# A mixer that begins with the memory's keys, its norm beside them, and low products that come last

## The chip, the cores and the metric

The kernel runs on one core of one Trainium2 chip. The metric is the time of one execution on the device, in microseconds (us), as the median of three runs. TensorE is called PE (its weight loads PEld), VectorE DVE, ScalarE ACT, GpSimd POOL and SyncE SP, as in the profile.

## What is computed

One inference step of a decoder trunk with two layers, in float32, for 256 prompt tokens and 8 x 8 sample tokens, which stand side by side as T = 320 columns. The model width is 1024, the hidden width of an FFN 2816, and there are 256 memory tokens, four heads, a pooling mixer in four groups and a causal depthwise convolution with 31 taps. The core of a layer:

```
x = x + 0.5 * swiglu_ffn(rmsnorm(x, ffn1_norm), ffn1_w_gu, ffn1_w_down)
h = rmsnorm(x, mix_norm)
u, v, q, gl = split(h @ w_in)
y_pool = pool_mixer(u)                # window means minus token, per-group map
a, gate = split(v);  z = a * sigmoid(gate)
y_conv = silu(layernorm(depthwise_conv31(z) + b_dw)) @ w_pw
k, v = split(rmsnorm(mem, mem_g) @ w_kv)        # keys and values of the memory
y_att  = cross_attend(q, k, v)
gates  = sigmoid(gl)                            # one per branch and channel
merged = gates[0]*y_pool + gates[1]*y_conv + gates[2]*y_att
x = x + merged @ w_out
x = x + 0.5 * swiglu_ffn(rmsnorm(x, ffn2_norm), ffn2_w_gu, ffn2_w_down)
```

A final RMSNorm follows. The sample group has cached keys, values, pool and conv states of its own; the new keys, values and states are outputs too.

## The kernel before

**Products in three parts.** Each operand is split into a high part (rounded to the type fp32r) and a low part, the rest. A product of a 128x128 block of weights with 320 columns of activations is three matmuls: high weight by high activation (L294), high weight by low activation (L295), low weight by high activation (L296). `chain` (L291) adds up such blocks in one PSUM bank, block after block, with the three parts of each block in turn. Banks are `mm` (three), `cv` and `st` (two each) and `sa`.

**Weights** come from DRAM in chunks of 1 MB, 16 blocks, on SP's queue, into four `raw` buffers, in the order that `stream_plan` lists; the memory tokens (`"m"`) and cached keys and values (`"k"`, `"v"`) have places in the same list. A *unit* is half a chunk: 8 blocks, 1024 columns. `Stream.split` makes its two halves `whi` and `wlo`: ACT casts `whi` (L224) and DVE subtracts for `wlo` (L116, the helper that issues all of DVE's work and all of POOL's arithmetic). While `share` is set, which is from the start of a mixer to ahead of `w_pw`, the second unit of each chunk goes another way: ACT casts `whi` (L217), ACT writes the rounded weights, negated, into `wlo` (L218), and a DMA from POOL's queue adds the weights themselves there, so that the low part stays (L219, `wlo<-in_w` in the trace). Four `whi` and four `wlo` buffers exist, and units are split three ahead of the one in use (`LA`).

**What runs beside the products.** At each new unit, `unit()` runs functions put off by `defer`, splits the next unit, and lets side tasks (generators begun by `start` with a rate) go on by so many steps. The convolution is the largest: 31 taps for each of 8 channel blocks on 256 columns and on the samples, on DVE, with a share on POOL and PE (`diag` products), paced at `RC` = 2.5 steps per unit. The tile scheduler then fixes the order in which each engine's instructions stand, from the order of the code, the waits and the buffers.

**The order of a mixer** before: `z` (16 units: for each of 8 blocks a chain for `a` and one for the gate, on an `h` that is multiplied by its weight but not yet by 1/rms, so that `rstd` is multiplied in after the bank, as `za` and `sgv`); beside it the statistics' product and rsqrt, and the memory operands `memh`, `meml` (`mem_operands`); the memory's keys (`kv_keys`, 8 units, result `kt`) and values (`kv_values`, 8 units, L457 on, line L471 for its low product) with `norm_gen` beside, which makes the normalised operands `hhi`, `hlo` of the rest; `q` (8 units); four pooling groups, with the attention's scores between them and the gates A; the gates C and B (8 units each; B's sigmoid is `sgb`, L847); the convolution's LayerNorm and SiLU (L566) and the operands `chi` (L567) and `clo`; the projection `w_pw` (8 units); and the output projection `w_out` (8 units) on the operands `mgh`, `mgl` of the merged branches. A mixer has 74 units ahead of `w_pw` in the stream. An FFN (`ffn`) has 44 units of gate and up products and 22 of the down product, and calls `on_block` as each block of the new `x` is done; at the end of FFN 1 that starts the norm's statistics and the operands of the un-normalised `h`.

In the profiled execution the mixer of layer 0 runs from 245.6 to 626 us (`z` to 312.6, keys to 343.4, the pooling groups from 402 to 503, gates C and B to 569, `w_pw` to 598), that of layer 1 from 1091.7 to 1476 us. The stretch from the start of `z` to the end of the pooling groups is called the stretch of the conv taps here.

## Time and profile before

| what | value |
|---|---|
| median of the three runs (lowest, highest) | 1725.13 us (1719.79, 1726.79) |
| profiled execution, its own time | 1725.18 us |
| its span in the trace | 1723.4 us |
| PE busy | 1654.5 us (96%) |
| DVE busy | 1119.0 us (65%) |
| ACT busy | 840.7 us (49%) |
| POOL busy | 319.8 us (19%) |
| DMA, mean of 16 engines | 187 GB/s |

Busy time counts an engine's instructions, which on PE overlap their successors, so that a busy PE is not PE at its best; what PE waits for, and the clock that it is granted (PEclk, 1.00 for 2.4 GHz), say more. Busy shares are means over stages with different limits: the four FFNs, some 230 us each, and the two mixers, 380 us each.

### The profile page before, as it was taken

Reading aid. Unit: us, or ns where it says so; the run is one execution under the profiler, and the core shown is the slowest. Engines: PE = TensorE matmul, PEld = TensorE weight load, DVE = VectorE, ACT = ScalarE, POOL = GpSimd, SP = SyncE. Lnnn points to the kernel's source line nnn. Section 1 sums busy time; section 2 is a strip of 40 time slices with the busy share of each in tenths; the row PEclk is TensorE's granted clock in tenths of the full one; section 3 lists DMA queues with packets and bytes.
Section 4 is the critical chain, followed back from the end, with each engine's and each line's share of the span. In section 5 each row is a group of like instructions: output and inputs, shape, how many; then the busy total and the mean of one; then the engine's idle time right before and its main releaser. Section 6 shows DMA issues by size and latency. Waiting matters only on the chain.

```text
span 1723.4 us, 27500 instructions
## 1 busy us (share of the span) xinstructions
PE 1654.5 (96%) x11194; PEld 1597.1 (93%) x11194; DVE 1119.0 (65%) x1822; ACT 840.7 (49%) x1267; POOL 319.8 (19%) x356
## 2 busy tenths in 40 slices
PE   8999998889999999999999999998899999999996
PEld 8999998879788999999999999997888899999996
DVE  7655449999754576564465555689995636755544
ACT  5444346656657354443344433555666664444432
POOL 2000005777410000000000000367762100000000
PEclk9999999999999999999999999999999999999999
DMA  7444457899899544444444444688888974444430
GB/s 266 147 147 152 152 185 214 219 256 253 251 293 273 176 151 155 147 147 148 147 147 150 153 155 154 180 230 230 227 266 269 311 208 161 147 150 154 155 129 31
DMA packets 51935, 322.52 MB, mean 187 GB/s; under 512 B 6240, under 2 KB 6304, under 8 KB 18656
## 3 DMA queue, kind: packets, MB, share of 16 engines
q1 hardware_dynamic: 38160, 270.75, 45.1%
q0 software_dynamic: 13360, 49.68, 13.5%
q8 instruction: 88, 1.44, 0.3%
q10 hardware_dynamic: 288, 0.33, 0.1%
q14 instruction: 39, 0.32, 0.1%
HBM read 311.91 MB, written 8.82 MB: 186 GB/s over the span
## 4 chain that ended last, share of the span: by engine, by line
PE 76%; DMA 9%; DVE 8%; issue 3%; POOL 2%; ACT 2%; DVEq 0%; SPq 0%; POOLq 0%; ACTq 0%
PE mm L296 17%; PE mm L294 17%; PE mm L295 17%; DMA wlo<-in_w 9%; PE cv L294 7%; PE cv L296 7%; PE cv L295 7%; DVE cv L116 3%; POOL pr L116 2%; DVE wlo L116 1%; PE sa L645 1%; DVE us L116 1%; PE st L825 1%; ACT wlo L218 1%; DVE hlo L116 0%
## 5 line engine op out<-in xcount | busy, mean ns | idle before, releaser
L224 ACT CAST whi<-raw 128x1024 fp32r<-128x1024 f32 (+1 forms) x371 | 388.3, 1047 | 601.5 <-PE mm L295 345.2
L116 DVE TENSOR_TENSOR wlo<-raw,whi 128x1024 fp32r<-128x1024 f32 (+1 forms) x371 | 465.3, 1254 | 242.5 <-ACT whi L224 241.6
L294 PE MATMUL mm<-hhi,whi 128*128 128x320 f32 x1736 | 547.0, 315 | 16.1 <-DVE sgv L116 9.6
L296 PE MATMUL mm<-hhi,wlo 128*128 128x320 f32 x1736 | 541.3, 313 | 16.4 <-DMA wlo<-in_w 16.3
L295 PE MATMUL mm<-hlo,whi 128*128 128x320 f32 x1736 | 542.0, 312 | 0.0
L294 PEld LDWEIGHTS mm<-hhi,whi 128*128 128x128 f32 x1736 | 329.3, 190 | 28.2 <-issue 15.5
L296 PEld LDWEIGHTS mm<-hhi,wlo 128*128 128x128 f32 x1736 | 328.9, 190 | 22.0 <-DMA wlo<-in_w 19.9
L295 PEld LDWEIGHTS mm<-hlo,whi 128*128 128x128 f32 x1736 | 329.4, 190 | 1.8 <-issue 0.4
L116 DVE SCALAR_TENSOR_TENSOR cv<-z,cst,cv 128x256 f32<-128x256 f32 x480 | 205.4, 478 | 3.4 <-ACT cv L484 1.4
L294 PE MATMUL cv<-hhi,whi 128*128 128x320 f32 x568 | 175.5, 309 | 0.0
L295 PE MATMUL cv<-hlo,whi 128*128 128x320 f32 x568 | 175.5, 309 | 0.0
L296 PE MATMUL cv<-hhi,wlo 128*128 128x320 f32 x568 | 175.5, 309 | 0.0
L116 POOL MEMSET z<- 128x120 f32 x4 | 0.8, 212 | 742.2 <-PE mm L295 742.2
L217 ACT CAST whi<-raw 128x1024 fp32r<-128x1024 f32 x74 | 77.5, 1048 | 120.3 <-PE mm L295 110.3
L294 PE MATMUL mm<-hidh,whi 128*128 128x320 f32 x418 | 129.2, 309 | 0.0
L295 PE MATMUL mm<-hidl,whi 128*128 128x320 f32 x418 | 129.2, 309 | 0.0
L296 PE MATMUL mm<-hidh,wlo 128*128 128x320 f32 x418 | 129.2, 309 | 0.0
L116 POOL TENSOR_TENSOR pr<-pr 128x512 f32<-128x512 f32 (+3 forms) x128 | 116.6, 911 | 6.6
L219 POOL DMA_DIRECT2D wlo<-in_w x74 | 64.6, 873 | 257.8 <-ACT wlo L218 188.5
L296 PEld LDWEIGHTS cv<-hhi,wlo 128*128 128x128 f32 x568 | 106.6, 188 | 0.0
L295 PEld LDWEIGHTS cv<-hlo,whi 128*128 128x128 f32 x568 | 106.6, 188 | 0.0
L294 PEld LDWEIGHTS cv<-hhi,whi 128*128 128x128 f32 x568 | 106.6, 188 | 0.0
(191 smaller groups left out, 2632.0 us busy)
## 6 DMA issues: line engine op xcount, KB each, us to landing
raw<-in_w SPq DMA_DIRECT2D x221, 1024.0 KB, 4.8
wlo<-in_w POOLq DMA_DIRECT2D x74, 512.0 KB, 8.9
raw<-in_kc SPq DMA_DIRECT2D x16, 1024.0 KB, 9.3
raw<-in_vc SPq DMA_DIRECT2D x16, 1024.0 KB, 8.7
out_co<-z POOLq DMA_DIRECT2D x16, 135.0 KB, 6.0
raw<-in_mem SPq DMA_DIRECT2D x2, 1024.0 KB, 4.8
out_mk<-kt POOLq DMA_DIRECT2D x2, 1024.0 KB, 9.4
out_mv<-va POOLq DMA_DIRECT2D x2, 1024.0 KB, 8.3
```

The costliest lines, as they stand in the source:

```text
L116: return op(*args, **kw)
L217: nc.scalar.copy(hi[:, :], raw)
L218: nc.scalar.mul(lo[:, :], raw, -1.0)
L219: nc.gpsimd.dma_start(lo[:, :], w_in[c][:, 1024:2048], accum_op=ALU.add)
L224: nc.scalar.copy(h, r)
L294: nc.tensor.matmul(out, hi, xh, start=(i == 0), stop=False)
L295: nc.tensor.matmul(out, hi, xl, start=False, stop=False)
L296: nc.tensor.matmul(out, lo, xh, start=False, stop=(i == len(xs) - 1))
L645: nc.tensor.matmul(po[32 * h:32 * h + 32, :256], pp[:, at:at + 32], raw[:, mb * 1024 + h * 256:mb * 1024 + h * 256 + 256], start=(bb == 0 ...
L825: nc.tensor.matmul(pv[:, :TP], vt[:, mb, o * P:o * P + P], kt[:, 2 * hd + mb, :], start=(mb == 0), stop=(mb == 1))
```

## The change

- The mixer begins with the memory's keys. `stream_plan` returns a list `seq` of chunks, in which the keys' four chunks stand ahead of those of `z`, and the values' behind; the memory tokens are loaded when FFN 1's down product begins, and their operands are made beside that product (`at_down`), with the subtraction on DVE where POOL had it.
- At the end of FFN 1 only the statistics are summed. `norm_gen` runs beside the keys from their third unit on, four steps a unit: DVE multiplies `x` by its weight and by `rstd` (`hf`), ACT casts `hhi`, DVE subtracts `hlo`.
- `z`'s chains take these normalised operands. The gate's sigmoid reads its bank, and `zfin` multiplies the other bank, which it holds until then, by the gate. `za`, the multiplications by `rstd` and the second set of operands are gone.
- In a chain all products with high halves of a unit come first, then those with its low halves; `kv_values` alike.
- While `share` is set, every third unit goes by way of the DMA, where it was every second: 48 such DMAs instead of 74 in the program, and 397 subtractions of `wlo` on DVE instead of 371.
- The pool `hp` goes, and the `big` buffers are eight instead of six.

Per mixer, DVE loses 16 multiplications by `rstd` and gains 8 `hf`; POOL loses 8 `hf` and 8 `meml`, and DVE gains the latter beside FFN 1. ACT has 26 loads of function tables instead of 34 in the program.

```diff
@@ -31,7 +31,7 @@
 NRAW = 4
 NW = 4
 LA = 3
-NBIG = 6
+NBIG = 8
 C_LEAD = 24
 RC = 2.5
 RS = 1.0
...
@@ -45,13 +45,24 @@
 C_ALL = C_ID + P
 
 
+LP = (2 * NJ * 24 + 720) // 16
+MP = NJ * 24 // 16
+
+
 def stream_plan():
 
+
     at = {}
+    seq = []
     nb = 0
     for l in range(L):
+        c = l * LP
+        seq += list(range(c, c + MP))
+        seq += list(range(c + MP + 8, c + MP + 12))
+        seq += list(range(c + MP, c + MP + 8))
+        seq += list(range(c + MP + 12, c + LP))
+        at.setdefault((nb + NJ * 16) // 16, []).append(("m", l))
         nb += NJ * 24
-        at.setdefault(nb // 16, []).append(("m", l))
         nb += 128 + 64 + 64 + 64
         for g in range(4):
             nb += 16 + (4 if g else 0)
...
@@ -209,14 +220,14 @@
             self.issue()
 
         def split(self, u):
-            c, half = divmod(u, 2)
+            c, half = seq[u // 2], u % 2
             raw = self.piece("w", c)[:, half * 1024:half * 1024 + 1024]
             hi = wp.tile([P, 1024], F32R, name=nm("whi"), tag="whi")
             lo = wp.tile([P, 1024], F32R, name=nm("wlo"), tag="wlo")
-            if self.share and half == 1:
+            if self.share and u % 3 == 2:
                 nc.scalar.copy(hi[:, :], raw)
                 nc.scalar.mul(lo[:, :], raw, -1.0)
-                nc.gpsimd.dma_start(lo[:, :], w_in[c][:, 1024:2048], accum_op=ALU.add)
+                nc.gpsimd.dma_start(lo[:, :], w_in[c][:, half * 1024:half * 1024 + 1024], accum_op=ALU.add)
             else:
                 n = 512 if u == 0 else 1024
                 for e in range(0, 1024, n):
...
@@ -289,12 +300,18 @@
     ws = Stream()
 
     def chain(out, xs, n):
-        for i, (xh, xl) in enumerate(xs):
-            hi, lo = ws.block()
-            nc.tensor.matmul(out, hi, xh, start=(i == 0), stop=False)
-            nc.tensor.matmul(out, hi, xl, start=False, stop=False)
-            nc.tensor.matmul(out, lo, xh, start=False, stop=(i == len(xs) - 1))
-            clk["pe"] += 3 * (3 + n / 2.4) * 1e-3
+
+        i, last = 0, len(xs) - 1
+        while i <= last:
+            m = min(8 - ws.blk % 8, last + 1 - i)
+            blocks = [(xs[i + e], ws.block()) for e in range(m)]
+            for e, ((xh, xl), (hi, lo)) in enumerate(blocks):
+                nc.tensor.matmul(out, hi, xh, start=(i + e == 0), stop=False)
+                nc.tensor.matmul(out, hi, xl, start=False, stop=False)
+            for e, ((xh, xl), (hi, lo)) in enumerate(blocks):
+                nc.tensor.matmul(out, lo, xh, start=False, stop=(i + e == last))
+            clk["pe"] += 3 * m * (3 + n / 2.4) * 1e-3
+            i += m
 
 
     def rsqrt_ops(ms, n, out, work=None):
...
@@ -349,8 +366,7 @@
         dve.tensor_tensor(out=lo, in0=src, in1=hi.bitcast(F32), op=ALU.subtract)
 
     def new_h():
-        return (hp.tile([P, KB, T], F32R, name=nm("hhi"), tag="hhi"),
-                hp.tile([P, KB, T], F32R, name=nm("hlo"), tag="hlo"))
+        return bigt([KB, T], F32R, "hhi"), bigt([KB, T], F32R, "hlo")
 
     rstd = const.tile([P, T], F32, name="rstd")
 
...
@@ -397,6 +413,8 @@
             defer(fin)
         flush()
         refs = [ref(j) for j in range(NJ)]
+        if at_down is not None:
+            at_down()
         for o in range(KB):
             pd = pwide()
             chain(pd[:, :T], refs, T)
...
@@ -417,16 +435,18 @@
         return h, st, on_block
 
 
-    def mem_operands(l, mh):
+    def mem_operands(l, box):
         raw = ws.piece("m", l)
+        mh = (bigt([KB, NM], F32R, "memh"), bigt([KB, NM], F32R, "meml"))
+        box.append(mh)
         if l == 0:
-            acc = tp.tile([P, T], F32, name=nm("macc"), tag="acc", bufs=1)
+            acc = t320("macc")
         for k in range(KB):
             src = raw[:, k * NM:(k + 1) * NM]
             f = t320("mf")[:, :NM]
             nc.scalar.mul(f, src, ccol(l, C_GK, k))
             nc.scalar.copy(mh[0][:, k, :], f)
-            pool.tensor_tensor(out=mh[1][:, k, :], in0=f, in1=mh[0][:, k, :].bitcast(F32), op=ALU.subtract)
+            dve.tensor_tensor(out=mh[1][:, k, :], in0=f, in1=mh[0][:, k, :].bitcast(F32), op=ALU.subtract)
             if l == 0:
                 if k == 0:
                     nc.scalar.activation(acc[:, :NM], src, AF.Square)
...
@@ -448,7 +468,7 @@
 
     def kv_keys(l, mh):
         for o in range(KB):
-            pk = pmm()
+            pk = pwide()
             chain(pk[:, :NM], [(mh[0][:, k, :], mh[1][:, k, :]) for k in range(KB)], NM)
             dve.tensor_tensor(out=kt[:, o, :], in0=pk[:, :NM], in1=rmem[:, :], op=ALU.mult)
         nc.gpsimd.dma_start(mk_out[l], kt[:, :, :])
...
@@ -660,34 +679,30 @@
             nc.scalar.copy(dst, tr[:, e * P:e * P + P].rearrange("p (h b t) -> p h b t", h=4, b=4))
         yield
 
-    def mixer(l, h, acc, on_block):
-        xs = hx(h)
-        box = []
-
-        def stat():
+    def mixer(l, mh, acc, on_block):
+        hn = []
+
+        def norm_gen():
             rsqrt_now(mean_bc(acc[:, :], T), T, rstd[:, :])
-
-        def norm_gen():
-            hn = new_h()
-            box.append(hn)
+            yield
+            hn.append(new_h())
+            hi, lo = hn[0]
             for k in range(KB):
                 hf = t320("hf")
-                nc.scalar.mul(hf[:, :], x[:, k, :], ccol(l, C_GM, k))
-                pool.tensor_tensor(out=hf[:, :], in0=hf[:, :], in1=rstd[:, :], op=ALU.mult)
+                dve.scalar_tensor_tensor(out=hf[:, :], in0=x[:, k, :], scalar=ccol(l, C_GM, k), in1=rstd[:, :],
+                                         op0=ALU.mult, op1=ALU.mult)
+                nc.scalar.copy(hi[:, k, :], hf[:, :])
                 yield
-                nc.scalar.copy(hn[0][:, k, :], hf[:, :])
-                dve.tensor_tensor(out=hn[1][:, k, :], in0=hf[:, :], in1=hn[0][:, k, :].bitcast(F32),
-                                        op=ALU.subtract)
+                dve.tensor_tensor(out=lo[:, k, :], in0=hf[:, :], in1=hi[:, k, :].bitcast(F32), op=ALU.subtract)
                 yield
 
-        defer(stat, 2)
         ws.share = True
         wide[0] = 0
+        defer(lambda: start("norm", norm_gen(), 4), 2)
+        kv_keys(l, mh)
+        drain("norm")
+        xs = hx(hn[0])
         z = [bigt([4, ZW], F32, "z") for _ in range(2)]
-        mh = (bigt([KB, NM], F32R, "memh"), bigt([KB, NM], F32R, "meml"))
-        va = bigt([2048 + KB * TS], F32, "va")
-        vt = va[:, :2048].rearrange("p (b c) -> p b c", b=2)
-        sgs = va[:, 2048:].rearrange("p (k t) -> p k t", k=KB)
         for i in range(2):
             pool.memset(z[i][:, :, 0:CB], 0.0)
             nc.gpsimd.dma_start(z[i][:, :, CB + T:ZW], sc_in[l, :, 4 * i:4 * i + 4, :])
...
@@ -698,29 +713,22 @@
             pg = pwide() if j < 2 else pmm()
             chain(pg[:, :T], xs, T)
             sg = t320("sgv")
-            za = t320("za")
-            dve.tensor_tensor(out=sg[:, :], in0=pg[:, :T], in1=rstd[:, :], op=ALU.mult)
-            nc.scalar.activation(sg[:, :], sg[:, :], AF.Sigmoid)
-            dve.tensor_tensor(out=za[:, :], in0=pa[:, :T], in1=rstd[:, :], op=ALU.mult)
-
-            def zfin(j=j, za=za, sg=sg):
+            nc.scalar.activation(sg[:, :], pg[:, :T], AF.Sigmoid)
+
+            def zfin(j=j, pa=pa, sg=sg):
                 zj = z[j // 4][:, j % 4, :]
-                dve.tensor_tensor(out=zj[:, CB:CB + T], in0=za[:, :], in1=sg[:, :], op=ALU.mult)
+                dve.tensor_tensor(out=zj[:, CB:CB + T], in0=pa[:, :T], in1=sg[:, :], op=ALU.mult)
                 nc.gpsimd.dma_start(co_out[l, :, j, :], zj[:, TP:TP + CB + CB * 8])
                 zdone.append(j)
                 if j == 0:
                     start("conv", conv_gen(l, z, zdone, ch, gate), RC)
 
             defer(zfin)
-            if j == 0:
-                start("mem", mem_operands(l, mh), 1)
+        va = bigt([2048 + KB * TS], F32, "va")
+        vt = va[:, :2048].rearrange("p (b c) -> p b c", b=2)
+        sgs = va[:, 2048:].rearrange("p (k t) -> p k t", k=KB)
+        kv_values(l, mh, vt)
         flush()
-        drain("mem")
-        start("norm", norm_gen(), 2)
-        kv_keys(l, mh)
-        kv_values(l, mh, vt)
-        drain("norm")
-        xs = hx(box[0])
 
         qa = bigt([KB * TP + KB * TS], F32, "qa")
         q = qa[:, :KB * TP].rearrange("p (k t) -> p k t", k=KB)
...
@@ -890,23 +898,22 @@
 
     mean = first_mean
     for l in range(L):
-        box = []
-
-        def ffn1_block(o, l=l, box=box):
+        acc, mbox, mem = [], [], []
+
+        def ffn1_block(o, acc=acc):
             if o == 0:
-                box.append(deferred_norm(l, C_GM))
-            box[0][2](o)
-
-        ffn(h, mean, ffn1_block)
-        h, st, _ = box[0]
-        mbox = []
+                acc.append(Stat())
+            acc[0].add(x[:, o, :])
+
+        ffn(h, mean, ffn1_block, lambda l=l, mem=mem: start("mem", mem_operands(l, mem), 1))
+        drain("mem")
 
         def mix_block(o, l=l, box=mbox):
             if o == 0:
                 box.append(deferred_norm(l, C_G2))
             box[0][2](o)
 
-        mixer(l, h, st.acc, mix_block)
+        mixer(l, mem[0], acc[0].acc, mix_block)
         h, st, _ = mbox[0]
         mean = lambda st=st: mean_bc(st.acc[:, :], T)
         if l + 1 < L:
```

Three places of the new order follow. `<-` stands between what an instruction writes and what it reads; the numbers at the names tell buffers apart.

On PE, the end of the last gate chain (a bank `mm`, read by `sgb`) and the start of the projection `w_pw` (operands `chi`, `clo`) in layer 0, before:

```order
L294 MATMUL mm_5654<-hhi_3112,whi_5546 128x320
L295 MATMUL mm_5654<-hlo_3113,whi_5546 128x320
L296 MATMUL mm_5654<-hhi_3112,wlo_5547 128x320
L294 MATMUL mm_5654<-hhi_3112,whi_5546 128x320
L295 MATMUL mm_5654<-hlo_3113,whi_5546 128x320
L296 MATMUL mm_5654<-hhi_3112,wlo_5547 128x320
L294 MATMUL mm_5699<-chi_5512,whi_5583 128x320
L295 MATMUL mm_5699<-clo_5513,whi_5583 128x320
L296 MATMUL mm_5699<-chi_5512,wlo_5584 128x320
L294 MATMUL mm_5699<-chi_5512,whi_5583 128x320
L295 MATMUL mm_5699<-clo_5513,whi_5583 128x320
```

and now:

```order
L309 MATMUL mm_5564<-hhi_2483,whi_5448 128x320
L310 MATMUL mm_5564<-hlo_2484,whi_5448 128x320
L312 MATMUL mm_5564<-hhi_2483,wlo_5449 128x320 x8
L309 MATMUL mm_5633<-chi_5572,whi_5486 128x320
L309 MATMUL mm_5668<-chi_5572,whi_5528 128x320
L309 MATMUL mm_5701<-chi_5572,whi_5565 128x320
L310 MATMUL mm_5633<-clo_5573,whi_5486 128x320
L309 MATMUL mm_5633<-chi_5572,whi_5486 128x320
```

Before, the three parts followed one another and `w_pw`'s first chain stood alone; now the eight low products stand together at the end of the chain, and three chains of `w_pw`, in the order of their operands, run through one another from its start.

On ACT, around the first of the eight sigmoids `sgb` of the gates B in layer 0, before:

```order
L218 ACTIVATE wlo_5404<-raw_5292 128x1024
L653 COPY exo_5410<-sa_5225 128x256
L224 CAST whi_5438<-raw_5302 128x1024
L847 ACTIVATE sgb_5399<-mm_5400 128x320
L660 COPY qa_3652<-st_5442 128x4x4x8 x2
L567 CAST chi_5512<-z_2371 128x320 x4
L567 CAST chi_5512<-z_2372 128x320 x4
L217 CAST whi_5473<-raw_5302 128x1024
L847 ACTIVATE sgb_5399<-mm_5437 128x320
```

and now, at the eighth (`z` here holds the convolution's result, whose SiLU is L566 before and L585 now):

```order
L855 ACTIVATE sgb_5284<-mm_5527 128x320
L235 CAST whi_5634<-raw_5292 128x1024
L855 ACTIVATE sgb_5284<-mm_5564 128x320
L585 ACT_TABLE_LOAD
L585 ACTIVATE z_2731<-z_2731,cst 128x320 x3
L586 CAST chi_5572<-z_2731 128x320
L585 ACTIVATE z_2731<-z_2731,cst 128x320
L586 CAST chi_5572<-z_2731 128x320
L585 ACTIVATE z_2732<-z_2732,cst 128x320
L586 CAST chi_5572<-z_2731 128x320
L585 ACTIVATE z_2732<-z_2732,cst 128x320 x3
L586 CAST chi_5572<-z_2731 128x320
```

All eight `chi` stood between the first and the second `sgb`; they now stand behind the eighth, with the load of the table and the SiLUs that they read.

On DVE, where the norm's `rstd` is ready at the start of the mixer of layer 0 (`cv` written by SCALAR_TENSOR_TENSOR are the taps, `macc` the memory's statistics), before:

```order
L116 SCALAR_TENSOR_TENSOR rstd<-rx_2417,rx_2416 128x320
L116 TENSOR_TENSOR sgv_2457<-mm_2412,rstd 128x320
L116 TENSOR_TENSOR za_2458<-mm_2380,rstd 128x320
L116 TENSOR_TENSOR macc_2472<-macc_2472,sq_2514 128x256
L116 TENSOR_TENSOR z_2371<-za_2458,sgv_2457 128x320
L116 SCALAR_TENSOR_TENSOR cv_2479<-z_2371,cst,cv_2479 128x256 x12
L116 TENSOR_TENSOR sgv_2550<-cv_2505,rstd 128x320
```

and now:

```order
L127 SCALAR_TENSOR_TENSOR rstd<-rx_2471,rx_2470 128x320
L127 TENSOR_TENSOR kt<-cv_2558,rmem 128x256
L127 TENSOR_TENSOR wlo_2598<-raw_2309,whi_2597 128x1024
L127 SCALAR_TENSOR_TENSOR hf_2485<-x,cst,rstd 128x320
L127 SCALAR_TENSOR_TENSOR hf_2489<-x,cst,rstd 128x320
L127 SCALAR_TENSOR_TENSOR hf_2526<-x,cst,rstd 128x320
L127 SCALAR_TENSOR_TENSOR hf_2530<-x,cst,rstd 128x320
L127 SCALAR_TENSOR_TENSOR hf_2564<-x,cst,rstd 128x320
L127 SCALAR_TENSOR_TENSOR hf_2568<-x,cst,rstd 128x320
L127 SCALAR_TENSOR_TENSOR hf_2604<-x,cst,rstd 128x320
L127 TENSOR_TENSOR kt<-cv_2596,rmem 128x256
L127 TENSOR_TENSOR hlo_2484<-hf_2485,hhi_2483 128x320
```

Where the first gate's `sgv`, `za` and taps followed `rstd`, the norm's eight `hf` and `hlo` follow it now, among the keys' `kt` and the low halves. The statistics' product that `rstd` comes from stands on PE inside the second chain of the keys.

## Rows read from the trace of the kernel before

**Rows 1.** The page: the span and PE's busy time.
```profile
span 1723.4 us, 27500 instructions
...
PE 1654.5 (96%) x11194; PEld 1597.1 (93%) x11194; DVE 1119.0 (65%) x1822; ACT 840.7 (49%) x1267; POOL 319.8 (19%) x356
```

**Rows 2.** Busy time by stretch: FFN, conv 0, keys, C and B, conv 1.
```profile
core 0: us, PE busy (x) PEld busy (x) DVE busy (x) ACT busy (x) POOL busy (x), PEclk, DMA share, GB/s
168.00:245.60 77.60, 77.60 (x531) 77.60 (x530) 37.33 (x45) 29.49 (x37) 1.83 (x4) 1.00 0.44 157
245.60:503.00 257.40, 236.76 (x1573) 216.24 (x1572) 216.28 (x417) 159.92 (x269) 145.38 (x159) 0.97 0.85 240
312.60:343.40 30.80, 25.62 (x194) 24.78 (x193) 28.93 (x55) 20.12 (x32) 23.67 (x24) 0.94 0.81 214
503.00:569.00 66.00, 63.38 (x464) 56.78 (x464) 31.28 (x62) 41.96 (x73) 6.02 (x7) 1.00 0.90 270
1091.70:1350.00 258.30, 235.23 (x1571) 215.75 (x1569) 212.37 (x400) 156.83 (x259) 145.79 (x155) 0.97 0.84 239
```

**Rows 3.** PE's waits, whole program: us in total, times, longest.
```profile
PE mm L296 <- DMA wlo<-in_w: 23.4, 17, 2.7
PE mm L294 <- DVE sgv L116: 9.6, 4, 3.8
...
PE mm L471 <- DMA wlo<-in_w: 6.5, 3, 3.2
...
PE mm L294 <- DVE kt L116: 3.5, 2, 2.2
PE mm L296 <- DVE wlo L116: 2.9, 1, 2.9
```

**Rows 4.** Busy time by stretch: sum of the seven at PEclk 0.50 or 0.51.
```profile
sum 34.00, PE 29.35 PEld 28.15 DVE 22.54 ACT 7.36 POOL 17.62; mean PE 4.19 PEld 4.02 DVE 3.22 ACT 1.05 POOL 2.52
```

**Rows 5.** Line L219, DMAs completing low halves: issue ns shortest/median/longest.
```profile
L219 POOL DMA_DIRECT2D wlo<-in_w x74: 847/867/1002, 248.0 to 1417.5; - x74
...
DMA to landing us min/median/max: 5.4/8.9/12.0
```

**Rows 6.** DVE's groups, 285:457, then 168:245.6: busy, mean ns | idle before.
```profile
L116 DVE TENSOR_TENSOR wlo<-raw,whi 128x1024 fp32r<-128x1024 f32 x21 | 28.2, 1343 | 4.7 <-ACT whi L224 4.6
L116 DVE TENSOR_TENSOR ysum<-ysum,z 128x320 f32<-128x320 f32 x5 | 8.3, 1664 | 0.0
...
L116 DVE TENSOR_TENSOR sgv<-mm,rstd 128x320 f32<-128x320 f32 x5 | 2.4, 476 | 0.0
...
L116 DVE TENSOR_TENSOR macc<-macc,sq 128x256 f32<-128x256 f32 x2 | 1.2, 610 | 0.0
...
L116 DVE TENSOR_TENSOR wlo<-raw,whi 128x1024 fp32r<-128x1024 f32 x22 | 26.9, 1224 | 29.6 <-ACT whi L224 29.6
L116 DVE SCALAR_TENSOR_TENSOR hlo<-x,cst,hhi 128x320 fp32r<-128x320 f32 x7 | 3.8, 549 | 2.5 <-ACT hhi L344 2.5
L116 DVE TENSOR_TENSOR acc<-acc,sq 128x320 f32<-128x320 f32 x6 | 2.9, 484 | 0.0
```

**Rows 7.** Timeline of ACT, 530 to 548 us: start, duration, instruction.
```profile
529.75 2.82 ACT L566 ACTIVATE z<-z,cst 128x320 f32<-128x320 f32 x5
...
534.39 1.28 ACT L566 ACT_TABLE_LOAD   x1
...
542.62 0.46 ACT L847 ACTIVATE sgb<-mm 128x320 f32<-128x320 f32 x1
...
544.63 2.99 ACT L567 CAST chi<-z 128x320 fp32r<-128x320 f32 x8 [0.99 <-DVE qa L116]
```

**Rows 8.** Timeline of PE and DVE, 595 to 602 us.
```profile
597.83 0.31 PE L294 MATMUL mm<-mgh,whi 128*128 128x320 f32 x1
...
599.02 1.23 DVE L116 TENSOR_TENSOR wlo<-raw,whi 128x1024 fp32r<-128x1024 f32 x1
...
600.16 0.48 DVE L116 TENSOR_TENSOR mgl<-merged,mgh 128x320 fp32r<-128x320 f32 x1
```

More of the change, by code (lines that the diff above doesn't have):

```diff
@@ L67, in stream_plan @@
         nb += NJ * 24
+    assert seq and nb == 16 * len(seq) and sorted(seq) == list(range(nb // 16))
     items = []
-    for c in range(nb // 16):
-        items += at.get(c, [])
+    for n, c in enumerate(seq):
+        items += at.get(n, [])
         items.append(("w", c))
-    return items
+    return items, seq
 @with_exitstack
@@ L96, in trunk_kernel @@
     wp = ctx.enter_context(tc.tile_pool(name="w", bufs=NW))
-    hp = ctx.enter_context(tc.tile_pool(name="h", bufs=1))
     big = ctx.enter_context(tc.tile_pool(name="big", bufs=NBIG))
@@ L160, in ccol @@
         return cst[:, c:c + 1]
-    items = stream_plan()
+    items, seq = stream_plan()
     class Stream:
@@ L171, in __init__ @@
             self.nsplit = 0
-            self.nunits = 2 * sum(1 for it in items if it[0] == "w")
+            self.nunits = 2 * len(seq)
             self.blk = 0
@@ L358, in hx, with ffn @@
         return [(h[0][:, k, :], h[1][:, k, :]) for k in range(KB)]
-    def ffn(h, mean, on_block):
+    def ffn(h, mean, on_block, at_down=None):
         xs = hx(h)
@@ L462, in kv_values @@
                 ws.blk += 8
-                for kk in range(2):
-                    k = 2 * kp + kk
-                    wh, wl = hi[:, kk * 512:kk * 512 + 512], lo[:, kk * 512:kk * 512 + 512]
-                    for mb in range(2):
-                        sh = mh[0][:, k, mb * P:mb * P + P]
-                        sl = mh[1][:, k, mb * P:mb * P + P]
-                        nc.tensor.matmul(pv[mb][:, :], sh, wh, start=(k == 0), stop=False)
-                        nc.tensor.matmul(pv[mb][:, :], sl, wh, start=False, stop=False)
-                        nc.tensor.matmul(pv[mb][:, :], sh, wl, start=False, stop=(k == KB - 1))
-                        clk["pe"] += 0.65
+                w4 = [(kk, mb) for kk in range(2) for mb in range(2)]
+                for kk, mb in w4:
+                    k, wh = 2 * kp + kk, hi[:, kk * 512:kk * 512 + 512]
+                    nc.tensor.matmul(pv[mb][:, :], mh[0][:, k, mb * P:mb * P + P], wh, start=(k == 0), stop=False)
+                    nc.tensor.matmul(pv[mb][:, :], mh[1][:, k, mb * P:mb * P + P], wh, start=False, stop=False)
+                for kk, mb in w4:
+                    k, wl = 2 * kp + kk, lo[:, kk * 512:kk * 512 + 512]
+                    nc.tensor.matmul(pv[mb][:, :], mh[0][:, k, mb * P:mb * P + P], wl, start=False, stop=(k == KB - 1))
+                    clk["pe"] += 0.65
             for mb in range(2):
```

## Prediction, made before the changed kernel ran

> **What bounds the kernel now.** I read the page first: TensorE (PE) is busy 96% of the span [rows 1], so only what it waits for, or does slowly, can be won. In the FFN it waits for nothing: 531 products in 77.6 us of unbroken work, 146 ns each [rows 2], so one unit of weights (8 blocks, 24 products) lasts 3.5 us. Next, PE's waits over the whole program [rows 3]. 29.9 us (23.4 + 6.5) are for low halves of weights that a DMA from POOL's queue completes (`wlo<-in_w`), in 20 pieces, the longest 2.7 and 3.2 us; 16.0 us (9.6 + 3.5 + 2.9) are for VectorE (DVE): two chains wait for a bank whose `sgv` waits for the norm, others for `kt` or a low half behind the conv taps. All of these lie in the two mixers. Third, the granted clock: seven stretches of 34.0 us together are at the lower level, 1.2 GHz, and PE is busy in 29.35 us of them [rows 4], half of which, 14.7 us or 2.1 us a stretch, is lost. They follow pauses of PE and so go with them. 29.9 + 16.0 + 14.7 = 60.6 us is what this change can reach. Last, the stretch of the mixers with the conv taps, 257.4 and 258.3 us: DVE is busy 84% and 82%, PE 92% and 91%, and in the keys alone DVE is at 94% while PE gets 83% [rows 2].
>
> **The change part by part.** The sum is made against the profiled execution, 1725.18 us (span 1723.4 and 1.8 around it); the median of the runs shown is 1725.13, so nothing has to be carried over.
>
> *Low products last.* Within a unit 16 products with the high half now come ahead of 8 with the low half, where the low half was needed by the third. It may come 14 products later, about 2.0 us (14 x 146 ns) [rows 2]. No product is added or removed, and the order's three kinds are spaced alike in the FFN, so PE pays nothing for the order itself. Against this, a PE that waits less also uses up its lead of three units faster: 74 units of a mixer now take 323.4 us (257.4 + 66.0) [rows 2], 4.4 us each, and without some 30 us of loss 4.0, which shortens the lead by 1.2 us. The net cover is about 0.8 us for a transfer that takes 5.4 to 12.0, typically 8.9 us to land [rows 5]. But the transfers are fewer: one unit in three instead of every second while they are shared, 48 instead of 74. Bounds: if each transfer costs PE what it costs now, 48 x 29.9 / 74 = 19.4 us stay; if the full 2.0 us counts for each of the 20 waits, whose mean is 1.5 us, only what sticks out of the longest, 2 us. 20 waits less 0.8 each leave 13.9, times 48/74 is 9. I take 8, as the DMA engines, busy 81 to 90% of these stretches, carry 13 transfers less in each mixer.
>
> *Keys first, operands made in the FFN.* The memory operands need ScalarE (ACT) for 16 instructions and now DVE for 8, while FFN 1's down product runs, where ACT works 29.5 and DVE 37.3 of 77.6 us [rows 2]; without that cover it would be 16 x 0.46 = 7 us of ACT. The operands of the un-normalised h (8 on each) go away there, so this is even. PE then has 64 blocks of keys to do while statistics, rsqrt and norm run, and no chain of the mixer waits for `rstd` in a bank any more: the 9.6 us go. Is the norm late instead? DVE has, behind the statistics' product (which stands 1.6 chains into the keys), 10 rsqrt instructions, 16 of the norm, 7 of `kt` and about 5 low halves: 33 x 0.48 + 5 x 1.22 = 22 us [rows 6]. The keys' other 6.4 chains have 24 products each of 122 ns (25.6 us less 6% of 30.8 for the clock, by 194) [rows 2], 18.8 us, and the last operand is needed 15 products of 146 ns later: 21 us. The norm is late by 1 us or, since DVE's instructions overlap a little, not at all: 0.5 a mixer, 1 in all; bounds 0 and 3 a mixer. Of the DMAs, the memory's load moves 176 blocks ahead on SP's queue, in front of weights that PE needs only units later; on POOL's queue the store of the keys moves 16 units ahead and the loads of the conv states behind the keys, still ahead of the first `z`. No PE wait hangs on them: 0.
>
> *DVE in the conv stretch.* Per mixer 13 low halves move from ACT and POOL to DVE (13 x 1.343 = 17.5 us), 8 norm products move from POOL (8 x 0.549 = 4.4), and 16 multiplications by `rstd` go (16 x 0.476 = 7.6) [rows 6]: +14.3. In layer 0 the memory's statistics leave the stretch as well, 7 additions and 10 rsqrt instructions at 0.61: -10.4. DVE then needs 220.2 us (216.3 + 14.3 - 10.4) in layer 0 and 226.7 (212.4 + 14.3) in layer 1. PE needs its busy time less 3% of the stretch for the clock: 236.8 - 7.7 = 229.1 and 235.2 - 7.7 = 227.5 [rows 2]. So DVE is filled to 96 and 99.6% of what PE leaves it. It is eased by a lead of three units and by POOL, which loses 16 instructions a mixer. While POOL works beside it a DVE instruction is longer: an addition of 320 columns that takes 0.48 us elsewhere has a mean of 1.66, the low half 1.343 instead of 1.224 [rows 6]. Bounds: 0, and all that would be lost if DVE cannot be packed closer than now (the rival below). I take 2 us in layer 0 and 4 in layer 1: 6 of the 16.0.
>
> The Trainium skill's page "SBUF — State Buffer", section "SBUF: two separate sides", says that DVE with two SBUF inputs and a GpSimd instruction that reads SBUF shut each other out for a whole instruction, and that a DMA issued from GpSimd can starve while DVE holds the ports; this speaks against moving work to DVE. The trace agrees on the instructions (0.48 against 1.66 us) but not on the issues of these DMAs, which take 847 to 1002 ns with no long one among 74 [rows 5]; by the rule alone my 6 us would be the rival's price instead.
>
> *The tail of the mixer.* The conv begins 8 units later and is paced by units, so its end moves against the projection `w_pw`. In ACT's order the 8 casts `chi` stood behind the first sigmoid of the last gate (`sgb`); now table load and SiLUs stand behind the eighth. They can start only when PE has ended its last chain before `w_pw`. From there: sigmoid 0.46, table 1.28, three SiLUs at 0.56, cast 0.37, together 3.8 us [rows 7], with two hand-overs 4.1 us in which PE has nothing to do. The fourth `chi` stands behind three more SiLUs (2.0 us) while PE has 9 products (1.3 us): 0.7 more, and 0.2 for the rest. 5.0 us a mixer, 10 in all; and a pause of 4 us is as long as the longest of [rows 3], so I add one stretch at the lower clock each, 4.2. DVE is ready by then: from the mean's product 26 instructions at 0.48 and 4 low halves, 17 us, against six chains of 3.5. Bounds: 3 us a mixer (fewer SiLUs ahead) and 8 (DVE late by 3).
>
> *Hand-overs.* With the high products first, a chain that follows its own operands reaches the last of them after 15 products (2.2 us), not 22 (3.2). The `mgl` of the last block ends at 600.64 us, 2.81 us after its chain began at 597.83 [rows 8]: 0.6 us late, at five such places (twice into the output projection, three times into an FFN). 0 if the low half ahead of it moves away, since high halves come free earlier; 3 at most. I take 2.
>
> *Sum.* 1725.2 - 60.6 + 8 + 6 + 10 + 4.2 + 2 = 1694.8, and 1 us for the norm in the keys: **1696 us**.
>
> **The rivals.**
> *The tail is hidden* (ACT is early, or PE's interleaved chains swallow it): 14.2 less, 1682 us. For it: before, nothing waits there. Against: the order on ACT is fixed and behind PE's own last chain.
> *The transfers still end last.* 19.4 instead of 8: 1707 us; with the waits for DVE that follow, up to 1715. For it: the lead shrinks as PE gains, and most transfers land just when they are used. Against: one third fewer.
> *DVE becomes the bound* (slower). DVE's share of the conv stretch stays at 84 and 82%, since its order is fixed and it must itself wait for ACT and PE: 220.2 / 0.84 = 262 and 226.7 / 0.82 = 276 us, 22 us more than now, where I have some 40 less. With the tail's 14.2 and the hand-overs' 2, less the 8 us of waits and clock behind the stretch: 1725 + 22 + 16 - 8 = 1755 us. It decides when DVE's share cannot pass 0.9. Against: it reaches 0.94 in the keys.
>
> **How the numbers follow.** Forecast 0.58 (its own range 1684 to 1707), hidden tail 0.14, transfers 0.20, DVE 0.08. Range: from the hidden tail with lower bounds of the rest, 1676, to the transfers with late DVE, 1716; above it lies the DVE case. 0.5%, 8.6 us, is about what a measurement of this kernel can tell from no change, so faster means below 1716.5: 0.58 + 0.14 + some 0.13 of the transfers' 0.20 = 0.85; same 0.08; slower 0.07.
>
> **What would show it.** In the profile after: PE's waits for `wlo<-in_w` at about 8 us and none over 2; none for `sgv`; a new wait for `chi` of about 4 us at two places, the largest left; DVE busy above 90% between keys and the third pooling map; few stretches at the lower clock, two of them behind `chi`. I am wrong if waits for DVE sum to more than 20 us, or if the waits for the transfers stay near 30.

## Result, and the profile after

The changed kernel took 1683.78 us (median of 4 runs, 1680.7 to 1684.46), the kernel before 1725.96 (4 runs): ratio 0.9757, 95% interval 0.9728 to 0.9786. The forecast was 1696 us, faster; the range 1676 to 1716 holds the result, which lies near its lower end. The profiled execution took 1683.86 us.

The page after, beside [rows 1]: the span is 41.3 us shorter, PE's busy time 14.0 us.

```profile
span 1682.1 us, 27304 instructions
...
PE 1640.5 (98%) x11194; PEld 1590.9 (95%) x11194; DVE 1122.7 (67%) x1832; ACT 796.4 (47%) x1201; POOL 278.3 (17%) x298
```

PE's waits after (us in total, times, longest), beside [rows 3]; L312 is now the low product of a chain, L490 that of the memory's values:

```profile
PE mm L309 <- ACT chi L586: 7.9, 2, 3.9
PE mm L309 <- ACT ut L770: 7.3, 5, 3.0
PE mm L490 <- DMA wlo<-in_w: 6.3, 2, 3.2
PE mm L309 <- ACT hhi L361: 5.8, 1, 5.8
PE sa L664 <- issue: 1.0, 2, 0.8
```

`sgv`, `kt` and the late subtractions are gone, the transfers' 29.9 us are 6.3, and `chi` is new, as nearly all of `ut` is (0.7 us before; `hhi` is the start of the program, the same in both). Busy time by stretch: the conv stretch of both mixers with the keys ahead of it, beside [rows 2].

```profile
core 0: us, PE busy (x) PEld busy (x) DVE busy (x) ACT busy (x) POOL busy (x), PEclk, DMA share, GB/s
246.35:481.35 235.00, 227.10 (x1569) 210.86 (x1567) 216.15 (x402) 138.17 (x223) 131.28 (x137) 0.99 0.79 240
...
1073.62:1309.00 235.38, 228.43 (x1568) 211.97 (x1567) 214.10 (x402) 137.95 (x223) 127.20 (x133) 0.99 0.78 238
```

They were 257.4 and 258.3 us; DVE's work in them is nearly unchanged, its share is now 92 and 91%. Five stretches are at the lower clock, together (beside [rows 4]):

```profile
sum 20.40, PE 19.80 PEld 15.84 DVE 15.46 ACT 12.94 POOL 8.09; mean PE 3.96 PEld 3.17 DVE 3.09 ACT 2.59 POOL 1.62
```

Half of PE's 19.80 us is lost by that clock, an estimate of 9.9 us where it was 14.7.

### The profile page after: what moved, and what is told of

Same layout as the page of the kernel before. It is cut to its first block, busy times and chain, and to the rows that moved or that the text cites. A ratio compares the mean times of both kernels' runs of the same rounds, so it can differ in the third digit from the quotient of the medians.

```text
span 1682.1 us, 27304 instructions
## 1 busy us (share of the span) xinstructions
PE 1640.5 (98%) x11194; PEld 1590.9 (95%) x11194; DVE 1122.7 (67%) x1832; ACT 796.4 (47%) x1201; POOL 278.3 (17%) x298
## 4 chain that ended last, share of the span: by engine, by line
PE 84%; DVE 10%; POOL 2%; ACT 1%; DMA 1%; issue 1%; DVEq 0%; SPq 0%; POOLq 0%; ACTq 0%
PE mm L309 19%; PE mm L310 19%; PE mm L312 19%; PE cv L310 8%; PE cv L309 8%; PE cv L312 8%; DVE cv L127 4%; DVE wlo L127 2%; POOL pr L127 2%; DVE us L127 1%; PE sa L664 1%; DMA wlo<-in_w 1%; PE st L833 1%; DVE ysum L127 0%; DVE pll L127 0%
## 5 line engine op out<-in xcount | busy, mean ns | idle before, releaser
L235 ACT CAST whi<-raw 128x1024 fp32r<-128x1024 f32 (+1 forms) x397 | 414.8, 1045 | 438.7 <-PE mm L310 255.9
L127 DVE TENSOR_TENSOR wlo<-raw,whi 128x1024 fp32r<-128x1024 f32 (+1 forms) x397 | 502.1, 1265 | 176.9 <-PE mm L312 70.0
L309 PE MATMUL mm<-hhi,whi 128*128 128x320 f32 x1712 | 512.5, 313 | 6.6 <-ACT hhi L361 5.8
L310 PE MATMUL mm<-hlo,whi 128*128 128x320 f32 x1712 | 509.0, 311 | 0.0
L312 PE MATMUL mm<-hhi,wlo 128*128 128x320 f32 x1712 | 288.4, 309 | 0.0
L312 PEld LDWEIGHTS mm<-hhi,wlo 128*128 128x128 f32 x1712 | 260.5, 188 | 0.3
L365 ACT CAST hidh<-up 128x320 fp32r<-128x320 f32 x88 | 40.0, 459 | 159.5 <-DVE up L127 159.5
L312 PE MATMUL cv<-hhi,wlo 128*128 128x320 f32 x592 | 98.8, 309 | 0.0
L312 PEld LDWEIGHTS cv<-hhi,wlo 128*128 128x128 f32 x592 | 89.9, 188 | 0.2
L127 DVE TENSOR_TENSOR up<-mm,rstd 128x320 f32<-128x320 f32 x53 | 26.0, 490 | 88.2 <-PE mm L312 88.2
L309 PE MATMUL cv<-hidh,whi 128*128 128x320 f32 x286 | 84.7, 309 | 0.0
## 6 DMA issues: line engine op xcount, KB each, us to landing
out_mk<-kt POOLq DMA_DIRECT2D x2, 1024.0 KB, 10.2
```

The source lines that it names most:

```text
L127: return op(*args, **kw)
L235: nc.scalar.copy(h, r)
L309: nc.tensor.matmul(out, hi, xh, start=(i + e == 0), stop=False)
L310: nc.tensor.matmul(out, hi, xl, start=False, stop=False)
L312: nc.tensor.matmul(out, lo, xh, start=False, stop=(i + e == last))
L365: nc.scalar.copy(hi, src)
```

## Experiments

### The three parts, one by one and in pairs

The change has three parts that can be had apart: the new order with its norm, low products last, and a third instead of half of the units transferred. In `b_low` and `b_third` one part is added to the kernel before, in `b_both` two; in `a_inter` and `a_second` one is taken out of the changed kernel, in `a_keys` two. The edits in their main lines, with - for the form before and + for the new one; the comments are mine, the products of the memory's values are reordered alike, and the source slice of the DMA goes with the condition:

```diff
 low products last (b_low, b_both; undone in a_inter, a_keys)
-        for i, (xh, xl) in enumerate(xs):    # hi*xh, hi*xl, lo*xh of each block
+            for e, ((xh, xl), (hi, lo)) in enumerate(blocks):    # hi*xh, hi*xl
+            for e, ((xh, xl), (hi, lo)) in enumerate(blocks):    # then lo*xh
 a third transferred (b_third, b_both; undone in a_second, a_keys)
-            if self.share and half == 1:
+            if self.share and u % 3 == 2:
```

Expected of `b_low`:

> The kernel before with nothing but the low products moved to the end of each unit (chains and the memory's values). Theory A, the place of the low product is what hides a transfer, its number counts in proportion: waits for the transferred low halves fall from 29.9 us to what the changed kernel has per transfer, 74 x 6.3 / 48 = 10 us, and with them some four of the seven stretches at half clock (8 us): 1697 us. Theory B, the number of transfers decides: the later place saves under 6 us of the waits, above 24 stay: 1718 us.

Expected of `b_third`:

> The kernel before with nothing but the transfers cut from every second to every third unit. Theory A: waits fall in proportion, to 29.9 x 48 / 74 = 19.4 us, and two stretches at half clock go (4 us): 1711 us, less if DVE's 13 more low halves a mixer are felt. Theory B: waits fall below 10 us, with four stretches at half clock: 1697 us.

Expected of `a_inter`:

> The changed kernel with the three products of each block in turn again. Theory A: waits for the transferred low halves rise from 6.3 to about 19 us and bring two or three stretches at half clock: 1684 + 13 + 5 = 1702 us. Theory B: they stay below 10 us: 1684 to 1688 us.

Expected of `a_second`:

> The changed kernel with every second unit transferred again (74 instead of 48). Theory A: waits for them rise in proportion, 6.3 x 74 / 48 = 9.7 us, and DVE, with 13 low halves less a mixer, lets go half of the 7.3 us that PE waits for ut: 1683 us. Theory B: waits rise to 20 us or more: 1698 us or more. If DVE's fullness is not behind the wait for ut, that stays at 7 us.

Expected of `a_keys`:

> The changed kernel with the three products of each block in turn and every second unit transferred, so that of the change the new order of the mixer and the norm beside the keys are left. If the parts add up as taken out one by one (5.4 and 10.5 us): 1700 us, with waits for transferred low halves at 16 to 20 us. If low products last and fewer transfers stand in for one another: waits near the 29.9 us of the kernel before, 1708 us or more.

Expected of `b_both`:

> The kernel before with low products last and every third unit transferred, without the new order. If the two add up as they did alone (15 and 16.5 us): 1694 us. If each takes away the same waits: waits for transferred low halves 3 to 6 us, waits for sgv, kt and ut 20 us or more as with each alone: 1703 us, and the new order is worth the 20 us from there.

| kernel | new order | low last | a third | median us | ratio to before (95%) | PE's waits for transfers | median landing | PE busy at the lower clock, us (stretches) |
|---|---|---|---|---|---|---|---|---|
| before | | | | 1725.96 | 1 | 29.9 | 8.9 | 29.4 (7) |
| b_low | | x | | 1710.77 | 0.9914 (0.9882, 0.9946) | 11.5 | 9.3 | 30.2 (8) |
| b_third | | | x | 1709.16 | 0.9904 (0.9875, 0.9933) | 10.2 | 7.9 | 32.0 (8) |
| b_both | | x | x | 1696.17 | 0.9845 (0.9814, 0.9875) | 7.5 | 7.7 | 13.6 (4) |
| a_keys | x | | | 1715.08 | 0.9959 (0.9935, 0.9983) | 18.2 | 9.0 | 19.6 (6) |
| a_second | x | x | | 1694.24 | 0.9822 (0.9791, 0.9853) | 16.9 | 8.9 | 24.1 (6) |
| a_inter | x | | x | 1689.21 | 0.9790 (0.9756, 0.9824) | 5.3 | 7.8 | 15.8 (4) |
| changed | x | x | x | 1683.78 | 0.9757 (0.9728, 0.9786) | 6.3 | 7.8 | 19.8 (5) |

Each ratio is against runs of the kernel before that were taken with that kernel: their median was 1725.7 us for `b_low`, `b_third`, `a_inter` and `a_second`, but 1722.8 for `b_both`, `a_rc275`, `a_ylast` and `a_keys` (whose ten runs lie between 1710.1 and 1724.7 us). So kernels are compared by their ratios.

PE's waits in `a_inter`, where the low half is again the third product of each block:

```profile
PE mm L305 <- ACT ut L765: 11.7, 5, 3.8
PE mm L305 <- ACT chi L581: 11.6, 2, 5.8
...
PE mm L485 <- DMA wlo<-in_w: 3.1, 2, 1.7
PE mm L307 <- DMA wlo<-in_w: 1.7, 2, 1.2
...
PE cv L307 <- DMA wlo<-in_w: 0.5, 1, 0.5
```

and the landing of the transfers, in `a_keys` (74 of them) and in `a_inter` (48):

```profile
DMA to landing us min/median/max: 6.0/9.0/12.1
```

```profile
DMA to landing us min/median/max: 5.1/7.8/12.1
```

and the stretches at the lower clock together, in `b_low`, where eight of them are left, and in `b_both`, where four are:

```profile
sum 34.00, PE 30.24 PEld 27.27 DVE 27.79 ACT 17.49 POOL 17.11; mean PE 3.78 PEld 3.41 DVE 3.47 ACT 2.19 POOL 2.14
```

```profile
sum 13.60, PE 13.58 PEld 12.36 DVE 11.79 ACT 5.84 POOL 8.51; mean PE 3.40 PEld 3.09 DVE 2.95 ACT 1.46 POOL 2.13
```

Most expectations held by half. `b_low`: the waits fell as theory A (the place of the low product hides the transfer, the number counts in proportion) had it, 11.5 us where it said 10, but the time was 1710.77 us where it said 1697, since no stretch at the lower clock went. `b_third`: the time was A's (1709.16 us, 1711 expected), the waits were nearly B's (10.2 us; A said 19.4). `a_inter`: B, with 5.3 us, and 1689.21 us just above its 1688. `a_second`: between the two, 16.9 us and 1694.24 us; its wait for `ut` fell from 7.3 to 2.9 us, as expected where DVE has less to do. `a_keys`: waits as if the parts added up (18.2 us), a time as if they stood in for one another (1715.08 us). `b_both`: a time near that of parts that add up (1696.17 us, 1694 expected), and waits of 7.5 us, a little above the 3 to 6 of parts that share them.

*The waits.* Each of the two parts alone takes away most of them, and together they give little more. They work at different ends, as an estimate from the traces shows in which each transfer is matched, by the order of the units, with PE's first low product of its unit (chains that run through one another blur this for up to one transfer in eight). From issue to that product it is a median of 9.2 us in the kernel before, 11.4 in `b_low`, 9.8 in `b_third` and 11.5 in the changed kernel; the landing takes 8.9, 9.3, 7.9 and 7.8 us. Low products last give a transfer some 2 us more time; fewer transfers land 1.0 to 1.6 us sooner, by the four pairs of the table. The median margin is 0.6 us before, 2.4 and 2.0 with one part alone, 3.6 in `b_both` and 3.9 in the changed kernel. Whether they land sooner for their number or for what goes with it (wider spacing, less work on ACT) no run separates.

*The time.* In the old order the two parts do nearly add up: 0.9 and 1.0% alone, 1.6% together, and the interval of `b_both` ends where those of the other two begin. What they share in waits is made good by the clock: each alone leaves eight stretches at the lower level, both leave four. `b_low` also hands part of its gain on: 18.4 us of waits for transfers go, about 15 us of time, and the waits for `ut` and `exo` rise from 0.7 us each to 4.9 and 4.3. Under the new order the two share more: from `a_keys`, 1.4 and 1.7% alone, 2.0% together. Low products last give 0.3% of that (0.9790 against 0.9757), which is not clear of noise, and what falls with them are the waits for `chi` and `ut`, not those for transfers. Last, the new order: 0.4% alone, 0.9% on top of the other two. Why 74 transfers cost 18.2 us under the new order and 29.9 under the old stays open.

### The wait for chi

> The changed kernel with the convolution paced at 2.75 steps a unit instead of 2.5, which puts chi between the third and the sixth sigmoid of the gates B on ACT. Theory D, the wait for chi is only a matter of that order: the 7.9 us and the two stretches at half clock behind them (5 us) go: 1671 us. Theory E, DVE is full in the conv stretch, so what the faster taps win at the end they lose before: waits for ut and kt grow by 8 us or more, 1680 us or more.

```diff
-RC = 2.5
+RC = 2.75
```

1678.9 us, 0.9741 (0.9715 to 0.9768). PE's waits:

```profile
PE mm L309 <- ACT ut L770: 7.0, 4, 3.0
...
PE mm L490 <- DMA wlo<-in_w: 5.9, 2, 3.3
PE mm L309 <- ACT sgb L855: 4.3, 2, 2.1
```

`chi` is gone, `ut` has not grown, so E falls and D holds for the wait; 4.3 of its 7.9 us come back for `sgb`, which now stands on ACT among the SiLUs. The clock gave nothing: there are still five stretches at the lower level, with PE busy for 18.97 us in them. So the median is 5 us lower where 13 were expected, and by the ratios, whose intervals overlap, even that is not clear of noise.

### The wait for ut

> The changed kernel with the last tap of each block writing the result where a copy on ACT took it from the bank, so that 16 such copies are gone. Theory F, PE waits for ut because ut stands on ACT behind such a copy, which waits for DVE's taps: the 7.3 us and two stretches at half clock (4 us) go: 1673 us; the waits for chi stay at 7.9 us. Theory G, ACT is late there for its softmax, behind DVE's maximum: ut stays above 5 us: 1681 us or more.

```diff
+                dst = acc[:, :TP] if k < TAPS - 1 else y[j][:, :TP]
-                dve.scalar_tensor_tensor(out=acc[:, :TP], ...
+                dve.scalar_tensor_tensor(out=dst, ...
-            nc.scalar.copy(y[j][:, :TP], acc[:, :TP])
```

1681.27 us, 0.9756 (0.9729 to 0.9783): no change, and `ut` 9.6 us in two waits. F falls; `ut` and the time are as G has them.

> The changed kernel with the prompt's scores of a group begun behind the two copies ut of that group, at two steps a unit, where they began ahead of them at one. Theory G, ut stands on ACT behind the exponentials, which wait for DVE's maximum among the taps: the 7.3 us of waits for ut fall below 2 us and the two stretches at half clock behind them go (4 us): 1673 us. Theory J, DVE's work is simply too much for these units, so that the wait only gets another name (plh, merged, kt or a low half): the sum of PE's waits stays within 3 us of the changed kernel's: 1681 us or more.

```diff
-            start("att", prompt_scores(q, g), 1)
             for i in range(2):
                 ...
                 nc.scalar.copy(ut[:, i, PB:PB + T], pu[:, :T])
+            start("att", prompt_scores(q, g), 2)
```

1689.21 us, 0.9797 (0.9761 to 0.9833): 5 us above the changed kernel in the median, though the intervals overlap. PE's waits, and one of ACT's:

```profile
PE mm L309 <- DVE merged L127: 8.5, 4, 2.2
PE mm L309 <- ACT chi L586: 7.9, 2, 3.9
...
PE mm L490 <- DMA wlo<-in_w: 5.6, 2, 2.9
PE st L629 <- ACT ex L606: 4.8, 6, 1.3
```

```profile
ACT ex L601 <- DVE mx L127: 14.7, 6, 5.8
```

G holds for the wait alone, J for the time: `ut` is gone, and 13.3 us under two other names are there, both behind DVE (`ex` by way of DVE's maximum `mx`). That is more than J's renaming: all of PE's waits come to 33.4 us where they were 28.8, and J had allowed 3 more.

### How full DVE can be

> The changed kernel with all low halves on DVE and no transfer for them: 24 more subtractions a mixer, some 16 of them (21 us) in the conv stretch, where DVE is busy 216.2 of 235.0 us. Theory H, DVE's share cannot pass what it is now, 0.92: the stretch grows to (216.2 + 21) / 0.92 = 258 us in each mixer, less the 6.3 us of waits for transfers: 1723 us. Theory I, DVE packs to nearly 1.0: the stretch is 238 us or little more, and the 6.3 us go: 1684 to 1692 us.

```diff
-        ws.share = True
+        ws.share = False
```

1691.87 us, 0.9809 (0.9780 to 0.9838). Busy time by stretch:

```profile
246.20:487.40 241.20, 233.39 (x1586) 215.04 (x1585) 227.29 (x407) 118.12 (x199) 107.42 (x102) 0.99 0.56 196
1079.00:1318.10 239.10, 231.65 (x1587) 215.28 (x1586) 226.93 (x407) 117.89 (x199) 105.97 (x98) 0.99 0.56 196
```

DVE reaches 94 and 95%; the stretches are 6.2 and 3.7 us longer, not 23. H falls and I holds, at the upper end of its range: the transfers' 6.3 us of waits are gone, others for DVE and ACT (`pll`, `clo`, `plh`) have come, and the median is 8 us higher. DVE's work is not free, but it is not the bound.

The Trainium skill's page "SBUF — State Buffer", section "SBUF: two separate sides", states that a DVE instruction with two SBUF inputs and a GpSimd instruction that reads SBUF shut each other out for a whole instruction. The traces agree, where little but the place of the inputs differs: in one stretch of the kernel before (layer 1), with POOL busy beside them, the products `z` of two SBUF tiles took 1039 ns in the mean and the products `za`, with one input in a bank, 477. The changed kernel's `z` reads a bank and takes 480. The Trainium skill's sentence there on starved DMAs speaks of DVE in a 2-port mode; no run here shows whether DVE was in one, so the issues of [rows 5] do not speak against it.

```profile
L116 DVE TENSOR_TENSOR z<-za,sgv 128x320 f32<-128x320 f32 x8 | 8.3, 1039 | 0.1
L116 DVE TENSOR_TENSOR za<-mm,rstd 128x320 f32<-128x320 f32 x8 | 3.8, 477 | 0.0
```

```profile
L127 DVE TENSOR_TENSOR z<-mm,sgv 128x320 f32<-128x320 f32 x7 | 3.4, 480 | 0.0
```

The low half did not lengthen further by the change: its mean in the two conv stretches is 1461 and 1452 ns, where it was 1376 and 1494.

### Both steps together

> Both steps on the changed kernel: the scores behind the copies, and the convolution at 3.0 steps a unit, which puts all chi between the first and the second sigmoid of the gates B, as in the kernel before. If G and D hold: no wait for chi, sgb or ut above 1 us, and only the 6.3 us for transfers and 1 for scores left: 1684 - 7.9 - 7.3 - 8 (four stretches at half clock) = 1661 us. If DVE's fullness gives it back in the conv stretch: 1672 us or more.

1678.12 us, 0.9727 (0.9696 to 0.9758): no wait for `chi`, `sgb` or `ut`, but 7.7 us for `merged` and 6.4 for `ex`, so that DVE gives it back, as the second reading has it. So the scores stay where they were, and the transfers of the memory's values go instead:

> The changed kernel with the convolution at 3.0 steps a unit, the scores begun where the changed kernel begins them, and no transfers while the memory's values are made (2 low halves more on DVE a mixer, where it is 25.05 of 25.09 us busy). If the order on ACT and the transfers are all that PE waits for there: no wait for chi, none for transfers, ut at the 7 us of the changed kernel, and four stretches at half clock instead of six: 1684 - 7.9 - 6.3 - 6 = 1664 us. If DVE must pay for it: waits for ut, kt, z or low halves by DVE grow by 6 us or more, 1671 us or more.

```diff
-RC = 2.5
+RC = 3.0
+        ws.share = False
         kv_values(l, mh, vt)
+        ws.share = True
```

1672.67 us (5 runs, 1671.93 to 1673.31), 0.9685 (0.9667 to 0.9703): the fastest, clear of the changed kernel. PE's waits:

```profile
PE mm L309 <- ACT ut L772: 7.1, 6, 2.6
...
PE mm L310 <- DVE pll L127: 4.0, 2, 2.6
PE mm L490 <- DVE wlo L127: 0.9, 2, 0.4
```

The waits for `chi` and for transfers are gone, and two stretches at the lower clock are left, 13.6 us together. 4.9 us for DVE (`pll`, `wlo`) are new, part of what it pays, and the time is that of the second reading (1671 us or more), not 1664. What each of the two edits gives was not run apart.

## Why the prediction was right, step by step

**The direction and most terms held; the base was too small.** Of the 60.6 us that I called reachable, 31.2 were to come back. The runs show 31.4 (transfers 6.3, `ut` 7.3, `chi` 7.9, clock 9.9), so by my terms the span should have shrunk by 29.2 us; it shrank by 41.3. The step that was mis-sized is "60.6 us is what this change can reach". It left out two things. Small waits outside [rows 3] came to 4.0 us and are now 1.0. And PE's idle time fell by 27.3 us (68.9 to 41.6), as its waits did, while its busy time fell by 14.0, of which the clock explains 4.8: a pause costs more than its idle time. The timeline of PE at a pause at full clock in the changed kernel shows it:

```profile
433.11 0.45 PE L312 MATMUL mm<-plh,wlo 128*128 128x320 f32 x2
433.96 0.42 PE L309 MATMUL mm<-plh,whi 128*128 128x320 f32 x1 [0.39 <-ACT ut L770]
434.21 0.31 PE L310 MATMUL mm<-pll,whi 128*128 128x320 f32 x1
```

The next product was due at 433.40 (two of 0.147 after 433.11) and came 0.56 us late, with 0.39 of idle; its successor came 0.25 after it, not 0.147. That is 0.27 us more than the idle time. Reckoned alike, the 28 pauses at full clock in the kernel before cost a mean of 0.28 us more. There are 11 pauses in the mixers where there were 33: an estimate of 22 x 0.27 = 6 us. The remaining 3 us of the 12 have no place yet.

**Transfers**: 8 forecast, 6.3 measured, a near number from terms that were off. The cover was right in kind, but I took 1.2 us off its 2.0 for a shorter lead, and that did not come: by the medians above it grew by 2.3 us (9.2, now 11.5). Nor do the waits go with the number, as `b_third` shows (10.2 us left, not 19.4). I had not thought of the earlier landing. "None over 2" was wrong: both are over 3 us, in the memory's values.

**Norm and hand-overs**: 1 and 2 us forecast, none seen. The operands made in the FFN cost 0.65 us at most: FFN 1's down product of layer 0 took 78.09 us after 77.44.

**DVE in the conv stretch**: 6 us forecast, 7.3 measured, as a wait for ACT that I did not foresee. The timeline of ACT and DVE at the longest:

```profile
405.40 0.68 DVE L127 TENSOR_REDUCE mx<-st 128x2 f32<-128x512 f32 x1
...
406.79 0.15 DVE L127 TENSOR_SCALAR mx<-mx 128x2 f32<-128x2 f32 x1
...
406.90 0.38 ACT L510 COPY z<-cv 128x256 f32<-128x256 f32 x1 [5.01 <-DVE cv L127]
...
408.24 1.28 ACT L601 ACT_TABLE_LOAD   x1
409.53 0.47 ACT L601 ACTIVATE ex<-st,mx 128x256 f32<-128x256 f32 x1
...
410.94 0.43 ACT L770 COPY ut<-mm 128x320 f32<-128x320 f32 x1
```

ACT idles 5 us for DVE's taps and then has the exponentials ahead of the copy that frees PE's bank. `a_ylast` shows that it is not this copy; with the exponentials moved, in `a_att`, the wait for `ut` goes, but not the loss. I put DVE's need in layer 1 at 226.7 us, 14.3 more than before; it was 214.1, only 1.7 more. 11 low halves came into the stretch, not 13 (+14.7 us), and the products `z` fell from 8.3 to 3.9 us, `hlo` and `ysum` by 4.8 together, which I had not counted. So 7.3 near 6 is partly luck. The rival (DVE as the bound, 1755 us) did not come.

**Tail**: the mechanism was right in its detail. The timeline of ACT behind the last gate chain of layer 0:

```profile
544.80 0.44 ACT L855 ACTIVATE sgb<-mm 128x320 f32<-128x320 f32 x1
545.26 1.28 ACT L585 ACT_TABLE_LOAD   x1
546.55 1.74 ACT L585 ACTIVATE z<-z,cst 128x320 f32<-128x320 f32 x3
...
548.20 0.44 ACT L586 CAST chi<-z 128x320 fp32r<-128x320 f32 x1
...
548.70 1.17 PE L309 MATMUL mm<-chi,whi 128*128 128x320 f32 x3 [3.93 <-ACT chi L586]
```

I had 4.1 us for this pause and 0.9 behind it; 3.93 came, and nothing separate behind it, where PE runs at the lower clock anyway. The rival "the tail is hidden" gave the nearer total, 1682, for a reason that did not happen.

**Clock**: two stretches forecast, 4.2 us; five came, 9.9 us, the others behind `ut` (two) and behind a transfer (one).

## What to carry to other kernels

Price a pause of the bounding engine above its idle time: here 0.27 us more for each, and five of the six pauses of about 3 us or more in the changed kernel came with a stretch at the lower clock. Two cures for one wait can share the wait and still add up in time, as other waits and the clock change with them, so run them apart and together, and judge by the time. Where an engine in the cover is as full as DVE here (92%), removing a wait behind it may only rename it (`ut`, then `merged` and `ex`); take work out of that stretch, or reorder the consumer's queue where a stage with idle time follows. An input that DVE reads from a PSUM bank instead of SBUF, while GpSimd works beside it, can halve an instruction (1039 and 480 ns).

## What was not expected of the hardware

The accumulating transfers land sooner when there are fewer: a median of 7.7 to 7.9 us with 48 of them, 8.9 to 9.3 with 74, in all eight kernels of the table. And DVE, which shared its stretch of 240 us with 107 us of POOL's work, was still busy for 94 to 95% of it.
